# The chunk recurrence of a state-space layer: from a serial chain of steps to a rotated prefix scan

## The chip, the cores and the metric

The kernel runs on one core of one Trainium2 chip. The metric is the device time of one execution in microseconds (us); lower is better. Its engines are TensorE (PE; PEld is its weight load), VectorE (DVE), ScalarE (ACT), GpSimd (POOL) and SyncE (SP), which here only issues DMAs. Each engine works through its own instructions in order and waits on semaphores for the others.

## The reference, cut to what matters

One inference step of a two-layer decoder: 256 prompt tokens and 8 sequences of 8 sample tokens, 320 columns in all, model width 1024. Each layer is FFN 1, a token mixer, FFN 2 and a per-layer input embedding. The token mixer runs sliding-window attention and, beside it, a state-space recurrence (S5) with 32 groups of 16 channels and 64 complex states each:

```python
a_bar = jnp.exp(lam * dt)                        # one complex number per state
bu = jnp.einsum('gnp,blgp->lbgn', b_bar, ug)     # inputs of the states
if h0 is not None:
    bu = bu.at[0].add(a_bar * h0)
_, h = lax.associative_scan(_ssm_combine, (a, bu), axis=0)   # h_t = a_bar h_{t-1} + bu_t
y = jnp.einsum('gpn,lbgn->blgp', c, h).real.reshape(bt, l, SSM_W)
```

## The kernel before, in words

Tokens are the columns, features the 128 partitions. Every weight block is loaded as f32, split into a high part (`wh`, on ACT, line 162) and a low part (`wl`, on DVE, line 163), and each product takes three matmuls of 320 columns (lines 181 to 183). Up to three weight blocks are ready ahead of their use.

The recurrence is cut into chunks of 8 tokens: 32 chunks of the prompt and 8 of the samples, one per sequence. `chunk_in(gb)` (op `i` in the order string) transposes the inputs `u2` of 8 groups and multiplies them with a table into `Vt`, which holds for each state (128 partitions: 64 real parts, then 64 imaginary parts), each of 32 groups and each of 40 chunks what the chunk adds to the state. Then the state at the start of each chunk, `H`, follows from H[c+1] = A H[c] + V[c], with A the eighth power of `a_bar`. `chunk_out(gb)` (op `y`) multiplies U and H with two tables, `tt` and `wc`, into the outputs. The sample chunks take their start from `h0`.

Before, `scan` (op `h`) does this for all 32 groups after the last `chunk_in`: the 32 prompt chunks form 4 blocks of 8; `astep` (lines 636 to 645) makes one complex step for all 4 blocks at once with five DVE instructions, seven times in a row, then three steps across the blocks, then ten instructions (lines 678 to 683) that bring the block starts into every chunk. The powers of A that it needs, `gr` and `gi` with nine entries each, come from `prep`.

`prep(l)` makes the tables of a layer. It is a generator: `step(side)` runs it to its next `yield` after each of the 22 hidden blocks and each of the 16 output blocks of an FFN, 38 times. Layer 0's tables are made during layer 0's FFN 1, layer 1's during layer 0's FFN 2; what is left is run at the FFN's end. Its last part is eight DMAs on POOL's queue (line 553) that lay out the `tt` table in DRAM.

The order of the work in the mixer is written out in `MIXSEQ`: `p` projections, `i` and `y` as above, `s`, `f`, `m` the scores, transposes and products of six attention units, `t` and `w` loads of `tt` and `wc`, `z` the embedding's projections, `A` and `S` the output products. A planner takes the instructions in this order of preference and puts each engine's instructions in sequence, by its own estimate of when each is ready. The row scale of a norm is a power on POOL (line 248), which the evacuations of the projections (lines 596, 600, 603) need.

Of the kernel before, what the change touches and what calls it, by code (L numbers as in the profile page):

```python
# [12 lines left out]
AF = mybir.ActivationFunctionType  # L13
# [6 lines left out]
P = 128  # L20
# [14 lines left out]
MIXSEQ = 'w0 p0 p1 p3 i0 p2 i2 w1 i3 i1 p8 h0 t1 p9 v t2 p5 t0 e x p4 y0 s0 s1 w2 f0 p6 m0 p7 s2 f1 t3 m1 s3 f2 m2 y0 w3 y0 y1 s4 f3 y1 m3 s5 z0 f4 z1 y1 z2 z3 y2 f5 y2 y3 m4 y3 y2 z4 y3 z5 z6 m5 a g0 g1 A0 z7 n A1 A2 S0 S1 S2 A3 S3'  # L35
SCANS = ((0, 32),)
# [3 lines left out]
FXG = 16  # L40
# [9 lines left out]
def hybrid_step_kernel(ctx: ExitStack, tc, I, O):  # L50
# [138 lines left out]
    class Norm:  # L189
        """Statistics and split operand of an RMSNorm over nb feature blocks."""  # L190
# [46 lines left out]
        def finish(self, then=None):  # L237
            """Statistics of the row scale; its broadcast is left for later, behind a few products."""
# [138 lines left out]
    def prep(l):  # L377
# [53 lines left out]
        V.tensor_tensor(pr[:, 1, :], t, er, op=OP.mult)  # L431
        V.scalar_tensor_tensor(t, sn, 2.0, cs, op0=OP.mult, op1=OP.mult)
        V.tensor_tensor(pi[:, 1, :], t, er, op=OP.mult)
        yield
        powers(pr, pi)
        gr, gi = st("gr", (P, 9, G)), st("gi", (P, 9, G))
        V.tensor_copy(gr[:, 1, :], pr[:, 8, :])
        V.tensor_copy(gi[:, 1, :], pi[:, 8, :])
        powers(gr, gi)
        V.tensor_scalar(gi[64:128], gi[64:128], -1.0, None, op0=OP.mult)  # L440
        gtab.append((gr, gi))
# [115 lines left out]
    def mix(l, pre, post):  # L557
# [71 lines left out]
        gr, gi = gtab[l]  # L629
# [3 lines left out]
        nc.sync.dma_start(h0, I["h0"][l])  # L633

        def astep(out, hin, vin, k, n, gs):
            GH = gs.stop - gs.start
            t = st("sc1", (P, 128))[:, : GH * n].rearrange("p (g n) -> p g n", n=n)
            w = st("sc2", (P, 128))[:, : GH * n].rearrange("p (g n) -> p g n", n=n)
            V.tensor_tensor(t, hin, gr[:, k, gs].unsqueeze(2).to_broadcast([P, GH, n]), op=OP.mult)
            for a, b in ((0, 64), (64, 0)):  # L640
                V.tensor_tensor(w[a : a + 64], hin[b : b + 64],  # L641
                                gi[b : b + 64, k, gs].unsqueeze(2).to_broadcast([64, GH, n]),
                                op=OP.mult)
            V.tensor_tensor(t, t, vin, op=OP.add)  # L644
            V.tensor_tensor(out, t, w, op=OP.add)

        def scan(hh):
            g0, GH = SCANS[hh]
            gs = slice(g0, g0 + GH)
            Hh, Vh = H[:, gs], Vt[:, gs]  # L650
            Hp = Hh[:, :, 0:32].rearrange("p g (b k) -> p g b k", k=8)
            Vp = Vh[:, :, 0:32].rearrange("p g (b k) -> p g b k", k=8)
            lc = st("lc", (P, G, 4))[:, gs]
            sb = st("sb", (P, G, 4))[:, gs]

            PO.memset(Hp[:, :, :, 0], 0.0)
            V.tensor_copy(Hp[:, :, :, 1], Vp[:, :, :, 0])
            for k in range(1, 7):
                astep(Hp[:, :, :, k + 1], Hp[:, :, :, k], Vp[:, :, :, k], 1, 4, gs)
            astep(lc, Hp[:, :, :, 7], Vp[:, :, :, 7], 1, 4, gs)  # L660
            V.tensor_copy(sb[:, :, 0:1], lc[:, :, 0:1])
            for b in range(1, 4):
                astep(sb[:, :, b : b + 1], sb[:, :, b - 1 : b], lc[:, :, b : b + 1], 8, 1, gs)
            for f0 in range(g0, g0 + GH, FXG):
                fs = slice(f0, min(f0 + FXG, g0 + GH))
                ng = fs.stop - f0
                fx = auxt("s", [P, 2, ng, 3, 8])
                ft, fw = fx[:, 0], fx[:, 1]

                def gk(tile, p0, p1):  # L670
                    return tile[p0:p1, 0:8, fs].rearrange("p k g -> p g k").unsqueeze(2).to_broadcast(
                        [p1 - p0, ng, 3, 8])

                def sk(p0, p1):
                    return sb[p0:p1, f0 - g0 : fs.stop - g0, 0:3].unsqueeze(3).to_broadcast(
                        [p1 - p0, ng, 3, 8])

                V.tensor_tensor(ft, gk(gr, 0, P), sk(0, P), op=OP.mult)
                V.tensor_tensor(fw[0:64], gk(gi, 64, P), sk(64, P), op=OP.mult)
                V.tensor_tensor(fw[64:128], gk(gi, 0, 64), sk(0, 64), op=OP.mult)  # L680
                V.tensor_tensor(ft, ft, fw, op=OP.add)
                Hf = H[:, fs, 8:32].rearrange("p g (b k) -> p g b k", k=8)
                V.tensor_tensor(Hf, Hf, ft, op=OP.add)
            S.activation(Hh[:, :, 32:NC], h0[:, gs], AF.Copy)
            S.activation(fin[:, gs, 8:9], sb[:, :, 3:4], AF.Copy)
# [25 lines left out]
        class Prompt:  # L711
# [42 lines left out]
            def mix(self):  # L754
# [7 lines left out]
                cp(ya[:, self.m, 0:TP], po[:, 0:TP])  # L762

        class Sample:
            """Four of the sample sequences."""

            def __init__(self, tp):
                self.tp = tp
# [381 lines left out]
```

## Time and profile before

| what | before |
|---|---|
| median of 3 runs | 1305.47 us |
| lowest and highest run | 1303.61 and 1311.94 us |
| span of the profiled execution | 1307.1 us |
| PE busy | 1272.5 us, 97% |
| DVE busy | 894.7 us, 68% |
| ACT busy | 599.1 us, 46% |
| POOL busy | 72.7 us, 6% |

The profiled execution has no time beside its span; the span lies inside the range of the three runs and 1.6 us above their median. Busy shares are means over the span. The mixer of layer 0 runs from about 254 to 374 us, that of layer 1 from about 895 to 1015 us; the rest is FFNs and embedding. [...]

### The profile page before, as it was taken

The page shows a single profiled execution, that of the slowest core. Times are in us where ns is not written, and L with a number is a line of the kernel's source. Part 1 is how long each engine was busy: PE and PEld are TensorE (multiplying, and loading weights), DVE is VectorE, ACT ScalarE, POOL GpSimd, SP SyncE. Part 2 cuts the span into 40 slices and gives each one's busy share as a digit, 9 for nine tenths or more (in the row PEclk, how much of TensorE's full clock was granted, in tenths as well). Part 3 has the DMA queues.
Part 4 walks back from the last instruction along what each step waited for, and adds up shares of the span by engine and source line. Part 5 has one row for each costly group of instructions (what it writes and reads, how often), then busy time and mean ns, then how long its engine had stood idle before and what let it go on. Part 6 is the DMA issues. An engine that isn't in the chain of part 4 may idle for free.

```text
span 1307.1 us, 22973 instructions
## 1 busy us (share of the span) xinstructions
PE 1272.5 (97%) x9153; PEld 1241.5 (95%) x9153; DVE 894.7 (68%) x1583; ACT 599.1 (46%) x986; POOL 72.7 (6%) x92
## 2 busy tenths in 40 slices
PE   7999999998999999999999999999899999999996
PEld 7999999987899999999999999999778999999996
DVE  6588885758896978656875555566778755555575
ACT  5433434543864443334653334345357544334453
POOL 4300001000004000100000000000000000000000
PEclk9999999997999999999999999999979999999998
DMA  7836766652254467754554455345322444454351
GB/s 259 307 115 202 249 208 206 194 168 84 76 179 146 138 209 252 233 180 137 169 172 146 125 165 162 123 138 185 130 81 84 147 147 140 134 178 147 110 179 41
DMA packets 74619, 210.62 MB, mean 161 GB/s; under 512 B 8544, under 2 KB 18496, under 8 KB 74480
## 3 DMA queue, kind: packets, MB, share of 16 engines
q1 hardware_dynamic: 72560, 203.22, 48.6%
q0 software_dynamic: 1664, 5.28, 1.2%
q8 instruction: 72, 1.18, 0.4%
q10 hardware_dynamic: 288, 0.66, 0.1%
q14 instruction: 35, 0.29, 0.1%
HBM read 191.78 MB, written 19.69 MB: 162 GB/s over the span
## 4 chain that ended last, share of the span: by engine, by line
PE 91%; DVE 5%; issue 2%; ACT 0%; DMA 0%; POOL 0%; SPq 0%; POOLq 0%; DVEq 0%
PE pt L181 17%; PE pt L183 17%; PE pt L182 17%; PE pc L181 10%; PE pc L183 10%; PE pc L182 10%; PE pa L844 1%; DVE sc L641 1%; DVE wl L163 1%; PE pa L624 1%; PE pa L613 1%; PE pt L725 1%; PE pa L499 1%; PE pt L750 0%; DVE sc L644 0%
## 5 line engine op out<-in xcount | busy, mean ns | idle before, releaser
L162 ACT ACTIVATE wh<-wr 128x1024 fp32r<-128x1024 f32 (+3 forms) x365 | 351.1, 963 | 562.1 <-issue 284.0
L181 PE MATMUL pt<-big,wh 128*128 128x320 f32 x1584 | 491.6, 311 | 1.0 <-ACT big L228 1.0
L182 PE MATMUL pt<-big,wh 128*128 128x320 f32 x1584 | 490.8, 310 | 0.0
L183 PE MATMUL pt<-big,wl 128*128 128x320 f32 x1584 | 490.5, 310 | 0.2 <-DVE wl L163 0.2
L163 DVE TENSOR_TENSOR wl<-wr,wh 128x1024 fp32r<-128x1024 f32 (+3 forms) x365 | 403.4, 1108 | 111.8 <-ACT wh L162 110.2
L181 PE MATMUL pc<-big,wh 128*128 128x320 f32 x992 | 314.0, 317 | 6.8 <-ACT wh L162 5.9
L183 PE MATMUL pc<-big,wl 128*128 128x320 f32 x992 | 310.4, 313 | 0.0
L182 PE MATMUL pc<-big,wh 128*128 128x320 f32 x992 | 310.3, 313 | 0.0
L181 PEld LDWEIGHTS pt<-big,wh 128*128 128x128 f32 x1584 | 297.8, 188 | 2.0 <-ACT big L228 1.5
L183 PEld LDWEIGHTS pt<-big,wl 128*128 128x128 f32 x1584 | 297.7, 188 | 0.8 <-DVE wl L163 0.6
L182 PEld LDWEIGHTS pt<-big,wh 128*128 128x128 f32 x1584 | 297.9, 188 | 0.4
L181 PEld LDWEIGHTS pc<-big,wh 128*128 128x128 f32 x992 | 188.9, 190 | 11.3 <-ACT wh L162 5.9
L182 PEld LDWEIGHTS pc<-big,wh 128*128 128x128 f32 x992 | 189.1, 191 | 1.4 <-DVE big L225 1.2
L183 PEld LDWEIGHTS pc<-big,wl 128*128 128x128 f32 x992 | 188.9, 190 | 0.8 <-DVE wl L163 0.4
L290 DVE TENSOR_TENSOR fa<-pt,ft 128x320 f32<-128x320 f32 x88 | 43.1, 490 | 98.1 <-PE pt L183 97.9
L287 DVE TENSOR_TENSOR ft<-pc,r 128x320 f32<-128x320 f32 x88 | 42.9, 490 | 58.5 <-PE pc L183 58.4
L248 POOL TENSOR_TENSOR r<-ms,mhalf 107x3 f32<-107x3 f32 x13 | 13.4, 1032 | 734.8 <-DVE ms L246 734.8
L333 DVE SCALAR_TENSOR_TENSOR fd<-pt,r 128x320 f32<-128x320 f32 x64 | 31.4, 490 | 32.8 <-PE pt L183 32.8
L294 ACT ACTIVATE big<-fa 128x320 fp32r<-128x320 f32 x88 | 40.5, 460 | 20.0 <-DVE fa L290 19.7
L288 ACT ACTIVATE ft<-ft 128x320 f32<-128x320 f32 x88 | 40.0, 457 | 19.9 <-DVE ft L287 19.9
L224 ACT ACTIVATE big<-xa,prm 128x320 fp32r<-128x320 f32 x64 | 35.3, 559 | 22.7 <-DVE xa L334 9.8
L295 DVE TENSOR_TENSOR big<-fa,big 128x320 fp32r<-128x320 f32 x88 | 42.7, 485 | 2.7 <-ACT big L294 2.7
(236 smaller groups left out, 893.6 us busy)
## 6 DMA issues: line engine op xcount, KB each, us to landing
wr<-f1u SPq DMA_DIRECT2D x44, 512.0 KB, 3.4
wr<-f2g SPq DMA_DIRECT2D x44, 512.0 KB, 3.4
wr<-f2u SPq DMA_DIRECT2D x44, 512.0 KB, 3.3
wr<-f1g SPq DMA_DIRECT2D x43, 512.0 KB, 3.4
wr<-f1d SPq DMA_DIRECT2D x32, 384.0 KB, 3.2
wr<-f2d SPq DMA_DIRECT2D x32, 384.0 KB, 3.2
wr<-f1d SPq DMA_DIRECT2D x32, 320.0 KB, 2.9
wr<-win SPq DMA_DIRECT2D x20, 512.0 KB, 4.0
```

Of the source, the lines that this page charges most:

```text
L162: S.activation(h[:, c], raw[:, c], AF.Copy)
L163: i = V.tensor_tensor(lo[:, c], raw[:, c], h[:, c].bitcast(F32), op=OP.subtract)
L181: PE.matmul(ps, h[:, c], xh, start=start and k == 0, stop=False)
L182: PE.matmul(ps, h[:, c], xl, start=False, stop=False)
L183: PE.matmul(ps, lo[:, c], xh, start=False, stop=stop and k == n - 1)
L224: S.activation(h, src, AF.Copy, scale=g)
L287: V.tensor_tensor(t, pg, r, op=OP.mult)
L288: S.activation(t, t, AF.Silu)
L290: V.tensor_tensor(a, pu, t, op=OP.mult)
L294: S.activation(h, a, AF.Copy)
L295: V.tensor_tensor(lo, a, h.bitcast(F32), op=OP.subtract)
L333: V.scalar_tensor_tensor(t, pd, 0.5, r, op0=OP.mult, op1=OP.mult)
```

## The change

The recurrence of the prompt chunks becomes one prefix scan per group on DVE (`tensor_tensor_scan`: state = decay * state + input, along the columns). A complex state can't go through it directly, so V is first turned by minus c times the phase of A for chunk c: in that frame the recurrence has the real factor |A|. The result is turned back into `H[c+1]`, and the last one into `fin`. `rotate(gb)` (op `r`) does this for 8 groups at a time, so that it can follow each `chunk_in`; `h0` in the order string is gone, and `r0`, `r2`, `r3`, `r1` stand behind `i2`, `i3`, `p8`, `r3`. The 8 groups lie one behind the other in a row of 256 columns, and the decay is 0 at the first column of each. The cosines and sines of c times the phase (`ect`, `est`, 32 chunks by 32 groups) and the decays (`dec`, filled on POOL) are made in `prep` by doubling, brought back to length 1 in two halves, and kept; the powers of A beyond the first are no longer made. `prep` gets six more `yield`s. The final states of the samples are made in one pass over 32 groups where there were two of 16. The builder is given `dynamic_dma_scratch_size=4096`. Comments are removed.

```diff
+MIXSEQ = 'w0 p0 p1 p3 i0 p2 i2 r0 w1 i3 r2 i1 p8 r3 r1 t1 p9 v t2 p5 t0 e x p4 y0 s0 s1 ...'
-MIXSEQ = 'w0 p0 p1 p3 i0 p2 i2 w1 i3 i1 p8 h0 t1 p9 v t2 p5 t0 e x p4 y0 s0 s1 ...'
...
         powers(pr, pi)
-        gr, gi = st("gr", (P, 9, G)), st("gi", (P, 9, G))
-        V.tensor_copy(gr[:, 1, :], pr[:, 8, :])
-        V.tensor_copy(gi[:, 1, :], pi[:, 8, :])
-        powers(gr, gi)
-        V.tensor_scalar(gi[64:128], gi[64:128], -1.0, None, op0=OP.mult)
-        gtab.append((gr, gi))
+        gr, gi = st("gr"), st("gi")
+        V.tensor_copy(gr, pr[:, 8, :])
+        V.tensor_copy(gi[0:64], pi[0:64, 8, :])
+        V.tensor_scalar(gi[64:128], pi[64:128, 8, :], -1.0, None, op0=OP.mult)
+        yield
+        for k in range(3):
+            V.tensor_tensor(er, er, er, op=OP.mult)
+        dec = st("dec", (P, G, NB))
+        PO.tensor_copy(dec, er.unsqueeze(2).to_broadcast([P, G, NB]))
+        PO.memset(dec[:, :, 0:1], 0.0)
+        ct_, sn_ = st("ect", (P, G, NB)), st("est", (P, G, NB))
+        PO.memset(ct_[:, :, 0:1], 1.0)
+        PO.memset(sn_[:, :, 0:1], 0.0)
+        for k in range(3):
+            V.tensor_tensor(t, us, us, op=OP.mult)
+            V.scalar_tensor_tensor(us, us, 2.0, uc, op0=OP.mult, op1=OP.mult)
+            V.tensor_scalar(uc, t, -2.0, 1.0, op0=OP.mult, op1=OP.add)
+        V.tensor_copy(ct_[:, :, 1], uc)
+        V.tensor_copy(sn_[:, :, 1], us)
+        yield
+        for m in (1, 2, 4, 8, 16):
+            n = min(m, NB - 1 - m)
+            shp = [P, G, n]
+            a1, a2 = ct_[:, :, m : m + 1].to_broadcast(shp), sn_[:, :, m : m + 1].to_broadcast(shp)
+            b1, b2 = ct_[:, :, 1 : n + 1], sn_[:, :, 1 : n + 1]
+            q1, q2 = auxt("s", [P, G, n]), auxt("s", [P, G, n])
+            q3, q4 = auxt("p", [P, G, n]), auxt("p", [P, G, n])
+            V.tensor_tensor(q1, a1, b1, op=OP.mult)
+            V.tensor_tensor(q2, a2, b2, op=OP.mult)
+            V.tensor_tensor(q3, a1, b2, op=OP.mult)
+            V.tensor_tensor(q4, a2, b1, op=OP.mult)
+            V.tensor_tensor(ct_[:, :, m + 1 : m + n + 1], q1, q2, op=OP.subtract)
+            V.tensor_tensor(sn_[:, :, m + 1 : m + n + 1], q3, q4, op=OP.add)
+            if m > 4:
+                yield
+        for c0 in (0, 16):
+            cc, ss = ct_[:, :, c0 : c0 + 16], sn_[:, :, c0 : c0 + 16]
+            q1, q2 = auxt("s", [P, G, 16]), auxt("p", [P, G, 16])
+            V.tensor_tensor(q1, cc, cc, op=OP.mult)
+            V.tensor_tensor(q2, ss, ss, op=OP.mult)
+            V.tensor_tensor(q1, q1, q2, op=OP.add)
+            V.tensor_scalar(q1, q1, -0.5, 1.5, op0=OP.mult, op1=OP.add)
+            V.tensor_tensor(cc, cc, q1, op=OP.mult)
+            V.tensor_tensor(ss, ss, q1, op=OP.mult)
+            yield
+        V.tensor_scalar(sn_[64:128], sn_[64:128], -1.0, None, op0=OP.mult)
+        gtab.append((gr, gi, ct_, sn_, dec))
         yield
...
-        def scan(hh):
...
+        PO.memset(H[:, :, 0:1], 0.0)
+        S.activation(H[:, :, NB:NC], h0, AF.Copy)
+
+        def rotate(gb):
+            gs = slice(gb * 8, gb * 8 + 8)
+            v = Vt[:, gs, 0:NB]
+            c, z = ect[:, gs], est[:, gs]
+            tg = auxt("s", [P, 3, 8, NB])
+            t, w, g = tg[:, 0], tg[:, 1], tg[:, 2]
+
+            def turn(src):
+                V.tensor_tensor(t, src, c, op=OP.mult)
+                V.tensor_tensor(w[0:64], src[64:128], z[64:128], op=OP.mult)
+                V.tensor_tensor(w[64:128], src[0:64], z[0:64], op=OP.mult)
+
+            turn(v)
+            V.tensor_tensor(t, t, w, op=OP.subtract)
+            V.tensor_tensor_scan(g.rearrange("p g c -> p (g c)"),
+                                 dec[:, gs].rearrange("p g c -> p (g c)"),
+                                 t.rearrange("p g c -> p (g c)"), 0.0, OP.mult, OP.add)
+            turn(g)
+            V.tensor_tensor(H[:, gs, 1:NB], t[:, :, 0 : NB - 1], w[:, :, 0 : NB - 1], op=OP.add)
+            V.tensor_tensor(fin[:, gs, 8:9], t[:, :, NB - 1 : NB], w[:, :, NB - 1 : NB], op=OP.add)
...
-            "p": proj, "i": chunk_in, "h": scan,
+            "p": proj, "i": chunk_in, "r": rotate,
...
-    nc = _bacc.Bacc("TRN2", target_bir_lowering=False, num_devices=1)
+    nc = _bacc.Bacc("TRN2", target_bir_lowering=False, num_devices=1,
+                     dynamic_dma_scratch_size=4096)
```

## Rows read from the trace of the kernel before

**Rows 1.** The page: the span, and PE's busy time, share, instructions.

```profile
span 1307.1 us, 22973 instructions
PE 1272.5 (97%) x9153; PEld 1241.5 (95%) x9153; DVE 894.7 (68%) x1583; ACT 599.1 (46%) x986; POOL 72.7 (6%) x92
```

**Rows 2.** Stretches of both mixers: start:end, length, busy by engine, clock, DMA.

```profile
270.00:286.00 16.00, 15.85 (x193) 13.73 (x192) 3.91 (x5) 8.47 (x16) 0.56 (x1) 1.00 0.62 203
286.00:322.00 36.00, 29.31 (x174) 25.98 (x173) 32.51 (x79) 8.91 (x15) 1.50 (x3) 0.81 0.23 73
300.50:307.50 7.00, 5.75 (x23) 5.18 (x24) 6.52 (x21) 0.00 (x0) 0.00 (x0) 0.53 0.25 77
314.50:321.20 6.70, 6.39 (x36) 5.00 (x37) 5.85 (x12) 0.98 (x2) 0.95 (x2) 0.50 0.07 10
322.00:354.00 32.00, 31.81 (x339) 26.66 (x338) 26.07 (x63) 28.41 (x85) 2.62 (x6) 1.00 0.29 99
925.00:968.00 43.00, 35.79 (x226) 31.79 (x225) 37.24 (x88) 12.97 (x31) 1.70 (x4) 0.80 0.28 95
940.00:946.50 6.50, 5.54 (x29) 5.33 (x30) 6.03 (x21) 0.81 (x1) 0.00 (x0) 0.74 0.25 83
952.60:965.40 12.80, 12.11 (x79) 9.73 (x80) 9.94 (x21) 5.00 (x19) 0.97 (x2) 0.51 0.24 84
```

**Rows 3.** PE's waits over the whole span: total us, times, longest.

```profile
PE pt L725 <- DVE big L600: 5.6, 2, 2.8
PE pa L844 <- DVE big L683: 5.3, 2, 2.9
PE pt L701 <- DVE kv L603: 3.0, 2, 1.5
```

**Rows 4.** Timeline of PE, layer 0: start, length, instruction, idle time before it and releaser.

```profile
301.75 1.23 PE L725 MATMUL pt<-kv,big 64*128 64x256 f32 x4 [2.82 <-DVE big L600]
...
314.81 0.65 PE L844 MATMUL pa<-wc,big 128*40 128x128 f32 x4 [2.39 <-DVE big L683]
```

**Rows 5.** Timeline of DVE, layer 0: start, length, instruction (first, one between, last).

```profile
285.83 0.29 DVE L657 COPY big<-big 128x128 f32<-128x128 f32 x1 [3.74 <-ACT big L83]
...
289.81 0.48 DVE L603 TENSOR_TENSOR kv<-pt,r 128x320 f32<-128x320 f32 x1
...
317.03 0.55 DVE L683 TENSOR_TENSOR big<-big,s 128x384 f32<-128x384 f32 x1
```

**Rows 6.** Timeline of ACT, layer 0: the first and last of four copies into `Vt`.

```profile
269.62 0.44 ACT L83 ACTIVATE big<-pa 128x320 f32<-128x320 f32 x1 [1.71 <-PE pa L624]
...
285.36 0.44 ACT L83 ACTIVATE big<-pa 128x320 f32<-128x320 f32 x1 [1.42 <-PE pa L624]
```

**Rows 7.** Groups of DVE instructions by shape: busy us, mean ns, idle before.

```profile
L359 DVE TENSOR_TENSOR cm<-pwr 128x32 f32<-128x32 f32 x1 | 0.2, 185 | 0.0
L739 DVE TENSOR_TENSOR s<-s,dn 128x256 f32<-128x256 f32 x4 | 1.7, 418 | 0.0
L463 DVE TENSOR_TENSOR sx<-kc,qr 128x512 f32<-128x512 f32 x1 | 0.7, 687 | 0.0
L857 DVE SCALAR_TENSOR_TENSOR big<-big,prm,pa 128x320 f32<-128x320 f32 x4 | 3.3, 816 | 0.6 <-PE pa L855 0.6
```

**Rows 8.** Stretches of the FFNs, columns as in Rows 2.

```profile
80.00:110.00 30.00, 30.00 (x209) 29.99 (x208) 29.81 (x93) 11.66 (x17) 0.00 (x0) 1.00 0.36 96
60.00:258.00 198.00, 198.00 (x1402) 196.30 (x1402) 154.79 (x303) 85.20 (x123) 5.63 (x10) 1.00 0.64 198
700.00:860.00 160.00, 160.00 (x1093) 160.00 (x1092) 85.45 (x116) 60.04 (x84) 0.00 (x0) 1.00 0.46 141
```

**Rows 9.** Timeline of POOL, layer 0, and landing times of line 553's DMAs.

```profile
209.00 4.85 POOL L553 DMA_DIRECT2D ttd<-ktd  x8 [8.42 <-DMA ktd<-kc]
260.99 0.88 POOL L248 TENSOR_TENSOR r<-ms,mhalf 107x3 f32<-107x3 f32 x1 [47.13 <-DVE ms L246]
DMA to landing us min/median/max: 3.2/5.8/6.2
```

More of the change, by code (lines that the diff above doesn't have):

```diff
@@ L34 @@
 WB = 4
-MIXSEQ = 'w0 p0 p1 p3 i0 p2 i2 w1 i3 i1 p8 h0 t1 p9 v t2 p5 t0 e x p4 y0 s0 s1 w2 f0 p6 m0 p7 s2 f1 t3 m1 s3 f2 m2 y0 w3 y0 y1 s4 f3 y1 m3 s5 z0 f4 z1 y1 z2 z3 y2 f5 y2 y3 m4 y3 y2 z4 y3 z5 z6 m5 a g0 g1 A0 z7 n A1 A2 S0 S1 S2 A3 S3'
-SCANS = ((0, 32),)
+MIXSEQ = 'w0 p0 p1 p3 i0 p2 i2 r0 w1 i3 r2 i1 p8 r3 r1 t1 p9 v t2 p5 t0 e x p4 y0 s0 s1 w2 f0 p6 m0 p7 s2 f1 t3 m1 s3 f2 m2 y0 w3 y0 y1 s4 f3 y1 m3 s5 z0 f4 z1 y1 z2 z3 y2 f5 y2 y3 m4 y3 y2 z4 y3 z5 z6 m5 a g0 g1 A0 z7 n A1 A2 S0 S1 S2 A3 S3'
 ABUFS = {"s": 2, "p": 2, "qs": 1, "kc": 1, "vc": 1, "sx": 2, "pj": 1}
@@ L39 @@
 KCUT = 7
-FXG = 16
+NB = 32
 HEAD = 2
@@ L430, in prep @@
         V.tensor_scalar(t, t, -2.0, 1.0, op0=OP.mult, op1=OP.add)
-        V.tensor_tensor(pr[:, 1, :], t, er, op=OP.mult)
-        V.scalar_tensor_tensor(t, sn, 2.0, cs, op0=OP.mult, op1=OP.mult)
-        V.tensor_tensor(pi[:, 1, :], t, er, op=OP.mult)
+        uc, us = st("uc"), st("us")
+        V.tensor_copy(uc, t)
+        V.tensor_tensor(pr[:, 1, :], uc, er, op=OP.mult)
+        V.scalar_tensor_tensor(us, sn, 2.0, cs, op0=OP.mult, op1=OP.mult)
+        V.tensor_tensor(pi[:, 1, :], us, er, op=OP.mult)
@@ L627, in chunk_in @@
             cp(Vt[:, gb * 8 : gb * 8 + 8, :], pv[:, : 8 * NC].rearrange("p (g c) -> p g c", g=8))
-        gr, gi = gtab[l]
+        gr, gi, ect, est, dec = gtab[l]
         H = bigt([P, G, NC])
@@ L633, in mix @@
         nc.sync.dma_start(h0, I["h0"][l])
[L635 to L645, printed above, removed]
@@ L647, in scan @@
-        def scan(hh):
[L648 to L685, printed above, removed]
@@ L923, in mix @@
             ops[o[0]](int(o[1:] or 0))
-        for f0 in range(0, G, 16):
-            fs = slice(f0, f0 + 16)
-            astep(fin[:, fs, 0:8], h0[:, fs], Vt[:, fs, 32:NC], 1, 8, fs)
+        shp = [P, G, 8]
+        ft = auxt("s", [P, 2, G, 8])
+        V.tensor_tensor(ft[:, 0], h0, gr.unsqueeze(2).to_broadcast(shp), op=OP.mult)
+        for a, b in ((0, 64), (64, 0)):
+            V.tensor_tensor(ft[a : a + 64, 1], h0[b : b + 64],
+                            gi[b : b + 64].unsqueeze(2).to_broadcast([64, G, 8]), op=OP.mult)
+        V.tensor_tensor(ft[:, 0], ft[:, 0], Vt[:, :, NB:NC], op=OP.add)
+        V.tensor_tensor(fin[:, :, 0:8], ft[:, 0], ft[:, 1], op=OP.add)
         PO.dma_start(O["hf"][l], fin)
```

## The prediction

> **What bounds the kernel now.** I began with the page's first part: PE is busy for 1272.5 of 1307.1 us [rows 1]. So the kernel is bound by TensorE nearly everywhere, and a change on DVE can win only where PE waits for DVE, or where those waits have cost PE its clock. PE's list of waits says where that is. Its three largest waits on DVE [rows 3] all lie in the mixers, once per layer each: for the evacuation of v's projection (line 603, 1.5 us), for that of q's (line 600, 2.8 us) and for the finished states (line 683, 2.9 us at most). None of the first two is long work by itself. DVE's timeline shows what stands in front of them: the scan runs from 285.83 to 317.58 us in layer 0, 31.7 us with other work threaded in, and line 603 sits in the middle of it [rows 5]. DVE is busy for 32.51 of the 36 us from 286 to 322, while ACT has 8.91 [rows 2]. So here DVE is the bound, not PE.
>
> The stretches of both mixers give the price. In layer 0, PE is idle for 36 - 29.31 = 6.7 us, in layer 1 for 43 - 35.79 = 7.2 us [rows 2]. [...] Work at half clock takes twice its time, so half of it is lost: about 2.8 + 3.2 = 6.0 us in layer 0. In layer 1 the first stretch is at half clock for only about half of its length: 5.54 x (1 - 0.74) = 1.4 us, and the second loses 12.11 x 0.49 = 5.9 us; 7.3 in all. The whole price of the scan's place is 6.7 + 6.0 + 7.2 + 7.3 = 27.2 us. That is the most that the removal can give.
>
> **The change, part by part.**
>
> *The scan itself.* One `rotate` has ten DVE instructions: three to turn, one subtraction, the prefix scan, three to turn back, one sum into H, one small sum into `fin`. Eight of them have 256 columns; the nearest row is 128x256 at 418 ns [rows 7], also for those of 64 partitions, since partitions run side by side. That is 8 x 0.418 = 3.3 us; the small one is 0.185 us at most, by the 128x32 row. The prefix scan has no row. Its lower bound is an ordinary instruction of its shape, 0.42 us; its upper bound is the slowest of like length in the mixer, 0.82 us for line 857 [rows 7]. I take 0.42, since shape and operands are those of that row. So a `rotate` is 3.9 us, up to 4.3, and four are 15.8 to 17.4 us, all instructions counted at full length.
> [...]
>
> *Its place.* The four copies into `Vt` come from 269.62 to 285.36 us [rows 6]. In the 16 us from 270 to 286 DVE is busy for only 3.91 [rows 2], so 12 us are free and three `rotate`s (11.8 us) fit there; a half of the third may slip behind. Behind the last copy at 285.8 stand `r1`, 3.9 us, and at most 2 us of leftover, instead of 31.7 us. DVE is then free from about 290 to 292. PE's wait for v ends as line 603 ends, at 290.3 [rows 5], so PE wants v from 288.8 on; its evacuation can be threaded into `r1`, as it was threaded into the scan. The waits on lines 600 and 683 ended at 301.75 and 314.81 [rows 4]: both go, since DVE is free 10 us before. What is late next in these places: v's evacuation, for which I keep 0.7 us of PE's wait per layer (between 0 and the 1.5 of today), and the attention units, whose chain of scores, exponentials and transposes now starts some 12 us earlier. From 322 to 354 PE is busy for 31.81 of 32 us, ACT for 28.41 and DVE for 26.07 [rows 2]: all three are nearly full there, but ACT had almost nothing to do in the 36 us before. PE's remaining projections now fill the time of the first unit's softmax. I keep 1.5 us per layer for gaps in it (between 0 and a whole lost wait of 2.8). Neither gap should lower the clock: the mean of 0.81 from 286 to 322 is a loss of 36 x 0.19 = 6.8 us, which the two stretches behind the waits of 2.82 and 2.39 us make up alone (7 x 0.47 + 6.7 x 0.5 = 6.6) [rows 2, 4]; the wait of 1.5 us cost none.
>
> *The tables.* Per layer `prep` loses the powers of `gr` (18 small instructions of 32 to 128 columns, 4.1 us between the rows) and gains three squarings, nine instructions of angle doubling, three copies (15 x 0.185 = 2.8 us), the doublings of 1, 2, 4, 8 and 16 columns by 32 groups (six instructions each, between the rows at about 0.185, 0.22, 0.28, 0.42, 0.66: 10.6 us), the renormalization (12 x 0.687 = 8.2 us [rows 7]) and a change of sign (at most 1.2 us). Net: 22.8 - 4.1 = 18.7 us of DVE in each of two FFNs. The FFN with layer 0's tables has DVE busy for 154.79 of 198 us [rows 8], so 43 us are free over its length. It is not spread evenly: from 80 to 110 DVE is full, 29.81 of 30 us, and yet PE loses nothing there and issues 209 matmuls in 30 us, 7.0 per us against 6.8 in a stretch without tables [rows 8]. Weight splits run three blocks ahead, three times 24 matmuls or 10 us, and that absorbs the lag. A hidden block takes 48 matmuls, 6.9 us; at the 53% of the table-free stretch (85.45 of 160 [rows 8]) DVE has 3.2 us of it left for a piece of `prep`. Today a piece of some 24 x 0.185 = 4.4, one of 8.5 and one of 7.5 us follow each other, and the lag grows to 1.2 + 5.3 + 4.3 = 10.8 us. After, pieces of 4.4, 4.6, 2.7, 6.6, 4.0, 4.1, 4.1, 1.2 and 7.5 us give 39.2 - 9 x 3.2 = 10.4 us; with five of them in output blocks, where I allow 0.8 us less room each, 14 us. I take no cost for PE. The cover is the weight queue, and if it fails it is the 3 to 4 us of difference and a fall of the clock worth 3 us: 0 to 7 us.
>
> *What the six yields move.* 38 steps no longer run `prep(0)` out, so its last DMAs are issued at FFN 1's end, and all behind the new steps comes six steps later. The eight DMAs of line 553 at 209.00 [rows 9] move by two hidden blocks of 6.9 and four output blocks of 30 matmuls, 4.3 us each: to about 240. On POOL's queue line 248 at 260.99 comes next, and the loads of `tt` on SP follow behind the rotations. With 4.85 us to issue and 6.2 us to land [rows 9] they end at about 251: free, with 10 us in hand for DVE's lag. SP's loads of the attention cache move by as much, into the last blocks of FFN 1, and are needed only by the attention units. The filling of `dec` on POOL has nothing behind it for 100 us.
>
> *Small things.* ACT loses one small copy; the sample's final states lose six instructions, off the path: 0.
>
> Sum on the profiled execution: 1307.1 - 27.2 + 2 x (0.7 + 1.5) = 1284.3 us. The span is 1.6 us above the median of the runs, so for a median I say **1283 us**.
>
> **The rivals.**
>
> *1. Another wait takes the place (20%).* The planner may put the rotations late, or in front of the u and v evacuations and weight splits that PE needs at once (a rotation queued before its copy into `Vt` holds up all behind it on DVE), and the attention units may keep PE waiting once per layer. For it: from 270 on DVE would be over 90% full, and ACT is at 28.41 of 32 us in the stretch that moves forward. Against it: PE has 7 us of projections to fill. Price: per layer one wait of 2.8 us and one half-clock stretch of 3.0 us stay, 11.6 us: about 1294.
>
> *2. Slower: the tables break the FFNs (9%).* DVE is already full from 80 to 110 us. If the lag passes what the prepared weights cover, PE waits for `wl` us for us: 2 x 18.7 = 37 us, and two or three falls of the clock of 3 us each: 45 us against 23 won, about 1328. It decides from a lag of 11 us on, which today's pieces reach without a loss. Against it: the new pieces are finer, and by the mean slack they end at 10.4.
>
> *3. POOL's queue (6%).* If the eight table DMAs are held up, line 248 behind them is late, and with it every projection of layer 0's mixer. One at a time, at 5.8 us each [rows 9], they would end 46 us after 240, 25 us behind line 248's time, and the clock falls once: about 1283 + 28 = 1311; two at a time they end at 263 and cost 2 us.
> [...]
>
> *4. It does not do what it says (4%).* Rotations all land behind 286 us and are as long as the scan: 1305.
>
> **The numbers.** My forecast has 61%, with a range of its own from 1276 (all 27.2 us, from the lowest run) to 1291 (7 us for the tables). Rival 1 reaches from 1288 to 1300. The range of 1276 to 1300 holds 61 + 19 and the milder half of rival 3, about 8 in 10. About 1% is what a measurement of this kernel tells from no change: below 1292.4 lie the forecast and half of rival 1: 0.71. Above 1318.5 lies rival 2: 0.09. The rest is 0.20.
>
> **What would show it.** In the profile after: ten DVE instructions per `rotate`, the prefix scan at 0.42 to 0.82 us; three rotations before 286 us; PE's waits on lines 600 and 683 gone and that on 603 at most 1.5 us; the granted clock at 1.00 from 286 to 322 and from 925 to 968; PE full in both FFNs with tables; line 553 done before line 248. It is wrong if PE waits for `wl` between 60 and 200 us, if line 248 starts late, or if a wait over 2.5 us turns up in the attention units.

## The result and the profile after

| | before | after |
|---|---|---|
| median of the runs on one chip (4 each) | 1306.97 us | 1290.94 us |
| lowest and highest | 1303.61, 1311.94 us | 1289.31, 1292.73 us |
| span of the profiled execution | 1307.1 us | 1290.9 us |

The ratio after/before is 0.9881, 95% interval 0.986 to 0.9903: faster by 1.2%, a small difference, but clear of 1. The time is 8 us above the prediction of 1283, at the upper end of the forecast's own range (1276 to 1291) and inside the whole range. The head of the page after (beside [rows 1]):

```profile
span 1290.9 us, 22996 instructions
PE 1260.0 (98%) x9153; PEld 1232.9 (96%) x9153; DVE 910.4 (71%) x1609; ACT 599.7 (46%) x984; POOL 78.0 (6%) x96
```

PE has lost 12.5 us of busy time with the same number of matmuls, and its mean granted clock over the span has risen from 0.985 to 0.992 (1.00 is full speed): fewer of them ran at half clock. DVE has become busier (910.4 us against 894.7) and the kernel faster: what counted was where its work stands. The line numbers have shifted: 248 is now 247, 553 is 595, 596, 600 and 603 are 638, 642 and 645. The stretches of [rows 2] and [rows 8] in the trace after:

```profile
254.00:286.00 32.00, 25.94 (x166) 24.21 (x166) 13.85 (x19) 11.34 (x14) 2.30 (x3) 0.88 0.50 178
286.00:322.00 36.00, 34.94 (x354) 30.75 (x352) 30.86 (x67) 18.63 (x43) 2.39 (x5) 0.97 0.38 123
...
925.00:968.00 43.00, 42.01 (x395) 37.30 (x393) 36.36 (x77) 29.09 (x80) 3.73 (x6) 1.00 0.36 127
60.00:258.00 198.00, 196.97 (x1395) 195.10 (x1393) 167.02 (x340) 83.63 (x121) 7.85 (x13) 1.00 0.60 194
375.00:640.00 265.00, 265.00 (x1865) 263.24 (x1864) 211.03 (x403) 118.06 (x172) 22.03 (x22) 1.00 0.57 188
```

Layer 1's stretch (the third line) is as forecast: PE 42.01 of 43 us at clock 1.00, where it had 35.79 at 0.80. Layer 0's mixer is nearly full from 286 on (34.94 of 36 us, 29.31 before), but has a new hole just before: 25.94 of 32 us at 0.88. Before, that stretch had none:

```profile
254.00:286.00 32.00, 31.69 (x331) 28.79 (x330) 12.58 (x17) 16.02 (x27) 2.62 (x4) 1.00 0.56 186
```

Both FFNs with tables (the last two lines of the block before) have DVE busier by 12.2 and 13.4 us (before, the second had 197.59). PE is full in the second and idle for 1.0 of 198 us in the first, at its very end: the table work is hidden. PE's waits (the four that matter):

```profile
PE pa L655 <- DVE big L638: 3.6, 3, 3.3
PE pc L180 <- ACT big L223: 3.4, 2, 2.0
...
PE pt L739 <- DVE big L642: 0.5, 1, 0.5
PE pt L715 <- DVE kv L645: 0.4, 1, 0.4
```

Of the three waits of [rows 3] one is gone and two are down to 0.5 us at most. Two others have come up, both in layer 0. To see what each stretch won or lost, take the starts of the row-scale power (line 247) in POOL's timeline. It runs once ahead of each part of a layer, so the distance of two of them is the time of a part. All runs that follow are in this table (us, from the profiled executions; the last column is the median of the runs). The ratios given with the runs are to the kernel before as it ran beside each (medians 1305.9 to 1309.3), and a run that adds or removes lines shifts the line numbers by a few.

| run | FFN 1, layer 0 | mixer, layer 0 | FFN 2, layer 0 | mixer, layer 1 | median of the runs |
|---|---|---|---|---|---|
| before | 236.4 | 137.2 | 239.8 | 139.4 | 1307 |
| after | 241.0 | 130.2 | 239.8 | 123.9 | 1290.9 |
| e1 tables early | 245.4 | 124.0 | 239.8 | 123.9 | 1291.5 |
| e2 six empty steps, before | 238.2 | 149.5 | 239.8 | 136.4 | 1318.3 |
| e3 Toeplitz on SP | 232.5 | 147.0 | 252.9 | 123.9 | 1313.6 |
| e4 reserve 8192 | 240.5 | 128.4 | 239.8 | 123.9 | 1290.0 |
| e5 six steps merged | 245.7 | 124.0 | 256.7 | 123.9 | 1307.0 |
| e6 the same, rotations called later | 245.4 | 123.9 | 256.2 | 123.8 | 1306.3 |
| e7 no Toeplitz DMAs, layer 0 | 236.5 | 124.3 | 239.8 | 123.9 | 1282.3 |
| e8 zero fill later | 236.4 | 124.0 | 239.8 | 123.9 | **1281.6** |
| e9 small Toeplitz rows | 237.2 | 124.3 | 239.8 | 123.9 | 1282.2 |
| e10 e8, rotations behind last copy | 236.4 | 132.3 | 239.8 | 132.0 | 1296.9 |
| e11 e8, rotations twice | 236.3 | 130.6 | 239.8 | 131.1 | 1295.1 |
| e12 both | 236.3 | 142.5 | 239.8 | 142.4 | 1318.1 |

Layer 1's mixer won 15.5 us. Layer 0's won only 7.0, and FFN 1 ahead of it lost 4.6: 2.4 us in all where 10.5 were forecast. That is the question of the experiments. The chain that layer 0 shows, first on POOL:

```profile
242.61 4.86 POOL L595 DMA_DIRECT2D ttd<-ktd  x8 [5.10 <-DMA ktd<-kc]
...
266.33 0.89 POOL L247 TENSOR_TENSOR r<-ms,mhalf 107x3 f32<-107x3 f32 x1 [18.69 <-DVE ms L245]
```

The Toeplitz DMAs come at 242.6 (predicted: about 240; before 209.0), and the power at 266.3 in place of 260.99 [rows 9]. Then the DMAs issued from 225 to 262 us (issues, KB of one, median us to landing):

```profile
wr<-win SPq DMA_DIRECT2D x8, 512.0 KB, 6.3
wr<-f1d SPq DMA_DIRECT2D x7, 320.0 KB, 4.2
...
kc<-kc SPq DMA_DIRECT2D x1, 512.0 KB, 9.8
...
ttd<-ktd POOLq DMA_DIRECT2D x1, 256.0 KB, 5.8
...
ttd<-ktd POOLq DMA_DIRECT2D x1, 32.0 KB, 8.3
```

In the same stretch before:

```profile
wr<-win SPq DMA_DIRECT2D x9, 512.0 KB, 4.2
wr<-f1d SPq DMA_DIRECT2D x6, 320.0 KB, 2.8
```

From 243 to 255 us the DMA engines are now full, a share of 1.00 at 354 GB/s, and ACT waits for both kinds of weights (its waits from 225 to 270 us):

```profile
ACT wh L161 <- DMA wr<-win: 4.4, 3, 2.3
...
ACT wh L161 <- DMA wr<-f1d: 3.7, 3, 2.0
```

One `win` block takes 9.5 us to land (before, at most 4.4). ACT's timeline has the wait for it:

```profile
255.06 1.06 ACT L161 ACTIVATE wh<-wr 128x1024 fp32r<-128x1024 f32 x1 [2.27 <-DMA wr<-win]
```

DVE splits that block at 256.15, in front of the residual sum that FFN 1's output is waiting for. PE's timeline shows where that ends:

```profile
258.95 0.41 PE L180 MATMUL pc<-big,wh 128*128 128x320 f32 x1 [1.98 <-ACT big L223]
...
276.55 0.44 PE L265 MATMUL pa<-ident,r 107*128 107x107 f32 x3
...
280.26 1.03 PE L655 MATMUL pa<-ident,big 128*40 128x128 f32 x8 [3.28 <-DVE big L638]
```

The first of these lines is FFN 1's loss: PE waits 1.98 and, a microsecond later, 0.59 us, and its mean clock is 0.81 from 258 to 267 us, where some 13 matmuls of 320 columns start 0.267 us apart in place of 0.147; that makes about 4.1 of the 4.6 us. The last is the hole in the mixer: u's evacuation (line 638) needs the row scale `r`, `r` needs the spread (line 265), and the spread stands in PE's order 57 matmuls later than before. The power was done at 267.2; PE ran the spread only at 276.55. Before, it came a microsecond behind the power:

```profile
262.84 0.44 PE L266 MATMUL pa<-ident,r 107*128 107x107 f32 x3
```

So PE waits for u, its clock falls (0.72 from 278 to 286, 0.85 from 286 to 294), and the first rotation starts at 287.9.

### The profile page after: what moved, and what is told of

It reads as the page before. It is cut to its first block, busy times and chain, and to the rows that moved or that the text cites. A ratio compares the mean times of both kernels' runs of the same rounds, so it can differ in the third digit from the quotient of the medians.

```text
span 1290.9 us, 22996 instructions
## 1 busy us (share of the span) xinstructions
PE 1260.0 (98%) x9153; PEld 1232.9 (96%) x9153; DVE 910.4 (71%) x1609; ACT 599.7 (46%) x984; POOL 78.0 (6%) x96
## 4 chain that ended last, share of the span: by engine, by line
PE 72%; DVE 3%; issue 2%; POOL 1%; ACT 1%; POOLq 0%; DVEq 0%; ACTq 0%
PE pt L180 14%; PE pt L181 14%; PE pt L182 14%; PE pc L180 9%; PE pc L182 9%; PE pc L181 9%; PE pa L858 1%; DVE wl L162 1%; POOL r L247 1%; PE pa L666 0%; PE po L773 0%; PE pa L869 0%; DVE s L690 0%; DVE s L689 0%; PE pt L764 0%
## 5 line engine op out<-in xcount | busy, mean ns | idle before, releaser
L293 ACT ACTIVATE big<-fa 128x320 fp32r<-128x320 f32 x88 | 40.4, 460 | 18.5 <-DVE fa L289 18.3
```

The costliest lines, as they stand in the source:

```text
L293: S.activation(h, a, AF.Copy)
```

## The experiments

My theory after the result (A): the six new yields push the last DMAs of layer 0's tables into the end of FFN 1, where they hold up weights and move the spread; the rotations themselves are as good in layer 0 as in layer 1. The rivals: B, the rotations, threaded between the copies, hold layer 0's mixer up; C, the smaller `dynamic_dma_scratch_size` holds POOL's DMAs up, a form of the prediction's third rival.

### e1: the tables as early as before

```diff
         if l == 0:
-            yield
-            yield
             zt = wpool.tile([P, 1024], F32, ...)
...
                 nc.sync.dma_start(tt_d[ll]..., zt...)
-                yield
...
             nc.sync.dma_start(sinks, I["sinks"])
-            yield
...
         PO.tensor_tensor(er, econ, zr, op=OP.pow)
         yield
         yield
-        yield
+        if l:
+            yield
```

> The changed kernel, but prep(0) gives up six of its older yields (two at its start, two in the loop that fills with zeros, one behind the masks, one of the three empty ones), so that everything behind the new tables is issued as early in FFN 1 as before the change; the tables and the mixer are those of the change. In this build's order the spread of the mixer's row scale stands 57 matmuls earlier on PE, where the kernel before has it. Theory A (six steps too late): layer 0 lost its gain because the last DMAs of the tables and of the attention cache ran into the end of FFN 1. Then the power of line 247 comes at about 261 (266.3 in the changed kernel), three rotations are done by about 288, the mixer's waits of 3.3 us and the fall of the clock from 278 to 294 go, and the time falls by 8 to 12 us to 1279 to 1283. Theory B (the rotations themselves, threaded between the copies and evacuations, hold layer 0's mixer up): about 1291, no change. [...] Against all: pieces of the tables that are now in the first, fullest blocks could make PE wait there, 3 to 7 us.

Measured: 1291.52 us, ratio to before 0.9889 (0.987 to 0.9908): no faster than the change. The median alone would have spoken for theory B. The parts say otherwise: layer 0's mixer takes 124.0 us, as layer 1's, and the waits there are gone, while FFN 1 takes 9 us more than before. That loss is at its start (a stretch):

```profile
30.00:60.00 30.00, 23.06 (x144) 22.40 (x144) 19.09 (x71) 11.12 (x16) 10.03 (x9) 0.89 0.90 323
```

The wait in PE's timeline:

```profile
43.80 0.63 PE L180 MATMUL pc<-big,wh 128*128 128x320 f32 x1 [6.58 <-ACT wh L161]
```

With 4 MB of zeros and the loads of the tables issued at once, PE waits 6.6 us for a weight. So B is refuted, and the first yields of `prep` turn out to be what keeps those 4 MB from standing in front of the weights.

### e2: six empty steps in the kernel before

```diff
         gtab.append((gr, gi))
         yield
+        for _ in range(6):
+            yield
```

> The kernel before, with nothing but six empty yields in prep where the change puts its six new ones. No table work is added and the scan is the old one. Theory A: the power of line 248 comes 4 to 6 us later than its 260.99, PE's order puts the spread 57 matmuls later, and the kernel is slower by 5 to 12 us: 1312 to 1319. Theories B and C: no change, 1307.

Measured: 1318.25 us, ratio 1.0097 (1.0079 to 1.0115), 12 us slower with nothing added but lateness. The power comes only 1.8 us later on FFN 1's own count; the expected 4 to 6 did not show. The mixer loses 12.4 us, and its spread runs at 272.22 (PE's timeline) against 262.84:

```profile
272.22 0.44 PE L266 MATMUL pa<-ident,r 107*128 107x107 f32 x3
```

The six steps alone cost the kernel before 12 us, three quarters of the 16 that the whole change gave. In the changed kernel the loss is smaller (about 10 us, e7 to e9); that its shorter DVE work makes up for a part is likely, but no run shows it.

### e3: the Toeplitz DMAs on SP's queue

```diff
-            PO.dma_start(dst[:, :, i * 16 :], src[:, :, : (8 - i) * 16])
+            nc.sync.dma_start(dst[:, :, i * 16 :], src[:, :, : (8 - i) * 16])
```

> The changed kernel, with the eight Toeplitz DMAs of line 595 issued on SP's queue instead of POOL's, as late as the change has them. POOL's queue then has nothing in front of the power of line 247, and in this build's order PE's spread stands 120 matmuls earlier than in the changed kernel; but the same bytes still move at the end of FFN 1, now in line with the weight loads. If the loss comes from POOL's queue and from the place of the spread that follows from it: 1281 to 1285. If it comes from the DMA engines being full at 243 to 255, so that the last weight loads are late: the mixer's weights are later still, PE waits at the start of the mixer, 1290 to 1296. Theory B: 1291.

Measured: 1313.59 us, ratio 1.0059 (1.0042 to 1.0076): worse than all of the expectations. The spread runs early, at 257.66, so its place does follow those DMAs. But PE now waits for a weight of the mixer (PE's timeline):

```profile
280.65 0.64 PE L182 MATMUL pt<-big,wl 128*128 128x320 f32 x1 [4.04 <-DVE wl L162]
```

It is not the weight's transfer that is late. The four `win` loads issued from 251.1 to 262.6 us land in 3.1 to 5.9 us, the last at 266.8. Their splits stand in ACT's order behind a copy that waits for PE's transposes (ACT's timeline):

```profile
271.07 1.07 ACT L82 ACTIVATE sx<-pa 40x512 f32<-40x512 f32 x2 [9.96 <-PE pa L655]
...
274.93 3.88 ACT L161 ACTIVATE wh<-wr 128x1024 fp32r<-128x1024 f32 x4
```

Layer 0's FFN 2, with layer 1's tables, loses 13 us in the same way: at its end, weights that landed 5 us and more before wait for their split behind other work of ACT. So the DMAs cost here through the order that the planner gives the engines, as with the spread, and the expectation that weights would land too late in the mixer did not show. FFN 1 and the mixer together take 379.5 us, 371.2 in the change; one by one they don't compare, since in e3 the power stands 48 matmuls earlier on PE.

### e4: 8192 bytes of DMA scratch

```diff
-                     dynamic_dma_scratch_size=4096)
+                     dynamic_dma_scratch_size=8192)
```

> The changed kernel with 8192 bytes in place of 4096 for the DMA scratch; every engine's order is the same. [...] Theories A and B: 1291, the issues at 4.86 us.

Measured: 1289.96 us, ratio 0.9879 (0.9862 to 0.9896); the change itself has 0.9881. The issues take 4.84 us against 4.86 (POOL's timeline):

```profile
241.80 4.84 POOL L595 DMA_DIRECT2D ttd<-ktd  x8 [5.36 <-DMA ktd<-kc]
```

By theory C the issues would get shorter or start earlier, the power would start before 266 us, and the time would fall by 3 us or more. With 8192 bytes they are 0.02 us shorter; they start 0.8 us earlier and the power 1.6 us (264.74), but in both traces what POOL waits for in front of them is `ktd`, whose wait is no shorter (5.36 us against 5.10), and the time is only 1.0 us lower, less than the spread of either kernel's runs. So theory C is out, and no run here shows a cost of 4096 bytes.

### e5 and e6: six steps merged, and the rotations called later

```diff
         PO.tensor_tensor(er, econ, zr, op=OP.pow)
         yield
-        yield
-        yield
...
         V.tensor_scalar(gi[64:128], pi[64:128, 8, :], -1.0, None, op0=OP.mult)
-        yield
...
         V.tensor_copy(sn_[:, :, 1], us)
-        yield
...
-            if m > 4:
+            if m > 8:
                 yield
...
         gtab.append((gr, gi, ct_, sn_, dec))
-        yield
```

> The changed kernel, with six yields of prep given back where they cost the start of the kernel nothing: two of the three empty ones behind the powers, and four of the new pieces of the tables joined to their neighbours (the one behind gi, the one behind the doubled angle, the one at m = 8, the one behind gtab); the first steps with their zero fill and loads stay where they are, and the pieces of DVE's work in the tables get larger. Both layers. Theory A (the last DMAs of the tables come six steps too late, and the run with everything early paid for its gain at 30 to 60 us): no wait at 30 to 60 us, line 247 at about 261, PE's 3.3 us wait before the mixer and the half clock behind it gone, 1279 to 1283. Theory D (whatever layer 0's mixer gains is lost again in FFN 1, since the table work must be done there anyway): 1288 to 1292.

e6 adds one more line:

```diff
-... p2 i2 r0 w1 i3 r2 i1 p8 r3 r1 t1 ...
+... p2 i2 w1 i3 i1 p8 r0 r2 r3 r1 t1 ...
```

> The kernel of the run before it in this list, with the four rotations called together where the scan was called (behind p8), instead of between the first projections and copies. Theory P (the early place gives most of the gain: the rotations run before v and q need DVE): the wait for v's evacuation and that for q's come back in part, 15.8 us of rotations stand in front of them, and each mixer loses 3 to 6 us: 1287 to 1293. Theory L (the shorter scan gives it, 17 us in place of 31.7, wherever it stands): within 2 us of that kernel, 1279 to 1285.

Measured: e5 1306.97 us, ratio 0.9989 (0.9974 to 1.0004); e6 1306.25, 0.9987 (0.9972 to 1.0002). The whole gain is lost, and neither of the times expected of e5 was met. Layer 0's mixer is whole (124.0 us), but the FFNs are not: 9 us in the one, 17 in the other. In both PE waits for weight splits, and once for a table instruction (`kk`) itself; FFN 2's waits (395 to 640 us, e5):

```profile
PE pt L182 <- DVE wl L162: 4.8, 1, 4.8
PE pt L180 <- ACT wh L161: 2.9, 3, 1.6
PE pc L180 <- DVE kk L409: 1.8, 1, 1.8
PE pc L182 <- DVE wl L162: 1.4, 1, 1.4
```

This is the mechanism of the prediction's second rival, which I gave 9%, at work as soon as the pieces are larger: the joined piece is 18 us by the prediction's own prices, past the 10.8 us of lag that by its estimate are borne without loss. So the yields were needed, and their number is what pushes the end back. e6 was to tell place from length and could not: the first prefix scan starts 11.4 us behind the power in both, because the planner puts a rotation where its copy is ready, whatever the order string says. e10 to e12 replace it.

### e7 and e9: without the transfers, or with small ones

```diff
-            PO.dma_start(dst[:, :, i * 16 :], src[:, :, : (8 - i) * 16])
+            if l or i == 7:
+                PO.dma_start(dst[:, :, i * 16 :], src[:, :, : (8 - i) * 16])
```

> The changed kernel without seven of the eight Toeplitz DMAs of layer 0 (the 16-wide one stays, so layer 0's tables of that kind are left mostly zero). The six steps stay late, and so do the loads of the attention cache; 1.1 of the some 10 MB that move from 225 to 262 us go, and POOL's queue is nearly free; in this build's order the spread of the row scale stands where the kernel before has it. If the late Toeplitz DMAs are the cause, the changed kernel's loss in layer 0 goes: 1279 to 1284, line 247 at 261 to 262. If it is the late loads of the cache and the weights behind them: 1288 to 1292, line 247 at 265 to 266.

```diff
-            PO.dma_start(dst[:, :, i * 16 :], src[:, :, : (8 - i) * 16])
+            PO.dma_start(dst[:, :, 112:], src[:, :, :16])
```

> The changed kernel with all eight Toeplitz DMAs of both layers still issued on POOL, 512 rows each, but each only 16 columns wide (so the tables are mostly zero): 0.26 MB in place of 1.15 MB per layer, with the same number of rows. In this build's order the spread of the row scale stands where the kernel before has it. If the loss in layer 0 comes from the bytes on the DMA engines, and from the place that the planner gives the spread because of their transfer time: 1279 to 1284. If it comes from POOL's issues (4.86 us) or from the number of rows: 1287 to 1291, and line 247 at 265 to 266.

Measured: e7 1282.27 us, ratio 0.9799 (0.9769 to 0.9829); e9 1282.15, 0.9799 (0.9771 to 0.9826). The six steps are as late as in the change, the cache loads too, and the loss is gone: the power is at 262.18 and 261.75, the spread back at 264.05 and 263.61 (PE's timeline of e7):

```profile
264.05 0.44 PE L265 MATMUL pa<-ident,r 107*128 107x107 f32 x3
```

That of e9:

```profile
263.61 0.44 PE L265 MATMUL pa<-ident,r 107*128 107x107 f32 x3
```

So the whole loss of layer 0 hangs on the late Toeplitz transfers, and in e9 on their size, not on POOL's issues or the number of rows. Two effects are left that these runs take away together: the weights that land late, and the place of the spread. The traces part them by time. FFN 1's 4.6 us arise before the power, which stands behind the same 1737 matmuls before and after, so the spread can't have made them: they are the weight that landed late. The mixer's other 6 us come behind it. In the runs that give the spread its old place and leave the rotations as they are, the mixer takes 123.9 to 124.3 us, also in e9, where `win` still lands only after 6.0 us; with the 57 matmuls in front it takes 128.4 (e4) and 130.2, and e2 has the same wait of 3.3 us. No run moves the spread alone, so this part is argued from the order of events.

### e8: the six steps from a place that costs nothing

```diff
-        if l == 0:
-            yield
-            yield
-            ...  (zero tile, zero fill of both layers, masks, with three yields)
         lam = st("lam", (P, 3, G))
...
         yield
         yield
-        yield
+        for _ in range(1 * l):
+            yield
...
         gtab.append((gr, gi, ct_, sn_, dec))
         yield
+        if l == 0:
+            zt = auxt("qs", [P, 512])
+            PO.memset(zt, 0.0)
+            nc.sync.dma_start(tt_d[0]..., zt...)
...
         V.tensor_copy(bst[64:128], bb[64:128, 1])
         yield
+        if l == 0:
+            nc.sync.dma_start(tt_d[1]..., zt...)
+            ...  (masks)
```

> The changed kernel with the pieces of the tables as the change has them, one DVE piece per step, but six steps given back at the front: the loads for the tables and the powers on POOL come first, without the two yields ahead of them, the zero fill of both layers' Toeplitz tables (4 MB) and the masks move from the start to two steps in the middle of FFN 1 (from a zero tile of 512 columns), and one of the three empty yields goes. Theory A, sharpened by the runs so far (late Toeplitz DMAs cost 8.7 us in layer 0; a crowded start costs 10; merged pieces of tables cost 5 us in one FFN and 17 in the other): none of the three prices is paid; no wait at 30 to 60 us, PE full from 60 to 240, line 247 at 261 to 263, layer 0's mixer 80 to 81 us long as layer 1's: 1279 to 1284. If DVE has no room for the tables so early, or the 4 MB are in the way of the weights at their new place: a wait of 3 to 7 us for wl or wh between 60 and 200 us, and 1285 to 1292.

Measured: 1281.56 us, ratio 0.9791 (0.9763 to 0.9818), with the full computation: the fastest kernel here, 2.1% under before and 0.9% under the change (0.9791/0.9881). DVE is full at the start and PE loses nothing by it; the stretch with the mixer's start is full too:

```profile
30.00:60.00 30.00, 30.00 (x207) 30.00 (x206) 29.49 (x110) 12.70 (x19) 8.68 (x11) 1.00 0.47 156
...
254.00:286.00 32.00, 31.66 (x330) 28.76 (x329) 22.59 (x42) 15.31 (x25) 2.30 (x3) 1.00 0.53 172
```

### e10 to e12: place against length

What in the scan was the price: that it stood behind the last copy, or that it was long? Two edits on e8, alone and together. The first makes every rotation depend on the last copy; the second does each rotation twice.

```diff
+        def tie(k):
+            V.tensor_scalar(ect[:, :, 0], Vt[:, 8, 0:G], 0.0, 1.0, op0=OP.mult, op1=OP.add)
-... i2 r0 w1 i3 r2 i1 p8 r3 r1 t1 ...
+... i2 w1 i3 i1 k r0 r2 r3 r1 p8 t1 ...
```

```diff
+            for _ in range(2):
-            turn(v)
+                turn(v)
...
```

> The kernel of run e8 with one small DVE instruction more per layer: it writes the ones in the cosine table's first column again, from a value that the last copy into Vt has brought, so that no rotation can begin before that copy; all four rotations then stand between it and the evacuation of v in DVE's order, in one stretch of 15.8 to 17 us. (Calling them later by name did not move them: in run e6 the planner put them where they were.) Theory P (the early place, between the copies, gives most of the gain): v's evacuation comes 10 to 12 us later, PE waits for it and for q's, with a fall of the clock, 3 to 6 us per mixer: 1288 to 1293 against e8's 1281.6. Theory L (DVE's shorter work gives it, wherever it stands): within 2 us of e8.

> The kernel of run e8 with each rotation done twice (same result): 33 us of DVE work per layer, about what the scan took (31.7 us with other work in it), but still in four parts that begin as soon as their copy is there. Theory P: most of the gain stays, since half of the work is done before the last copy: within 4 us of e8. Theory L: the gain goes, each mixer is back at 90 to 96 us, 1300 to 1310.

> Both: rotations twice and none before the last copy. DVE's work is as long and stands where the scan of the kernel before did. By both theories the gain goes: each mixer 94 to 98 us as in the kernel before, 1306 to 1312. If it stays under 1295, neither length nor place was what the scan cost.

Measured: e10 1296.93 us, ratio 0.9903 (0.9889 to 0.9918); e11 1295.08, 0.9891 (0.9876 to 0.9906); e12 1318.14, 1.0066 (1.0049 to 1.0082). Per mixer, against 124.0: 8.2 us for the place, 6.8 for the length, 18.5 for both. Each theory expected one of the two to be nearly free; neither is. DVE's timeline says why. v's evacuation, in e8 behind the third rotation:

```profile
284.58 0.69 DVE L693 TENSOR_TENSOR_SCAN s<-dec,s 128x256 f32<-128x256 f32 x1
...
288.39 0.49 DVE L644 TENSOR_TENSOR kv<-pt,r 128x320 f32<-128x320 f32 x1
...
290.27 0.68 DVE L693 TENSOR_TENSOR_SCAN s<-dec,s 128x256 f32<-128x256 f32 x1
```

The same evacuation in e10:

```profile
299.06 0.47 DVE L644 TENSOR_TENSOR kv<-pt,r 128x320 f32<-128x320 f32 x1
```

And PE's timeline of e10, with the wait for it:

```profile
299.59 0.90 PE L717 MATMUL pt<-ident,kv 128*128 128x128 f32 x3 [3.68 <-DVE kv L644]
```

DVE's timeline of e11:

```profile
298.85 0.49 DVE L644 TENSOR_TENSOR kv<-pt,r 128x320 f32<-128x320 f32 x1
```

PE's of e11:

```profile
299.40 0.90 PE L715 MATMUL pt<-ident,kv 128*128 128x128 f32 x3 [3.67 <-DVE kv L644]
```

Two different edits put v's evacuation off by nearly the same time (10.7 and 10.5 us) and cost PE the same wait, 3.7 us, and 8.2 and 6.8 us in all. Behind the wait PE's clock is at 0.50 (e10, a stretch):

```profile
300.00:306.00 6.00, 6.00 (x28) 5.22 (x27) 5.09 (x10) 1.21 (x3) 0.76 (x2) 0.50 0.28 94
```

In e12 it is no longer v but q's evacuation, with twice the work in front of it, that PE waits for, 10.2 us (line 641 there; PE's timeline):

```profile
313.86 0.63 PE L180 MATMUL pc<-big,wh 128*128 128x320 f32 x1 [10.16 <-DVE big L641]
```

So the gain of the change is neither "fewer instructions" nor "earlier" by itself. It is that DVE is free when PE asks for v and q.

## Why the prediction was right, and where its sum was wrong

*The price of the scan's place, 27.2 us: right, and a little short.* The clock is back at 1.00 in layer 1, and the waits of [rows 3] are gone or at most 0.5 us. In e8, free of the side effect, the mixers are 13.2 and 15.5 us shorter than before, 28.7 in all, where 27.2 was called the most that the removal can give; the span is 27.3 us below before (1279.8 against 1307.1). e12, with rotations that are late and twice as long, gives it all back and 9 us more. Its DVE work is longer than the scan's: the rotations add up to 33.7 us in a mixer, the scan's 63 instructions to 24.5 (31.7 was its length with other work threaded in). The clock's part of the price was counted from the four short stretches of [rows 2], as if work at half clock took twice its time. That factor was an estimate, and no run shows it: back-to-back matmuls of 320 columns (lines 181 to 183 of the kernel before) start 0.147 us apart at a clock of 1.00 (from 100 to 105 us) and 0.267 at 0.50 (from 305 to 307), 1.8 times.

*What takes the place, 4.4 us: too much.* v's wait in layer 1 is 0.4 us, where 0.7 was kept; none of PE's waits for the attention units is longer than 0.5 us, where 1.5 us of gaps were kept. Layer 1's mixer won 15.5 us where 12.3 were forecast.

*A rotation, 3.9 us: slightly short.* The groups of DVE instructions, eight of each:

```profile
L694 DVE TENSOR_TENSOR_SCAN s<-dec,s 128x256 f32<-128x256 f32 x8 | 5.5, 684 | 0.2
...
L688 DVE TENSOR_TENSOR s<-big,ect 128x256 f32<-128x256 f32 x8 | 3.4, 425 | 9.1 <-ACT big L82 9.0
...
L689 DVE TENSOR_TENSOR s<-big,est 64x256 f32<-64x256 f32 x8 | 3.4, 420 | 0.1
...
L699 DVE TENSOR_TENSOR fin<-s 128x8 f32<-128x8 f32 x8 | 1.4, 170 | 0.0
```

I took 0.42 us for the prefix scan; it takes 0.684, so a rotation is 4.2 us, inside the bound of 4.3, and four are 16.9. That the scan costs no more than an ordinary instruction of its shape was my assumption, and it did not hold: it takes 1.6 times a product. That an instruction on 64 partitions costs what one on 128 does held: 420 ns against 425. The scan's 0.26 us change about 0.3 us per layer.

*Tables at no cost: right.* FFN 2 takes 239.8 us before and after, and FFN 1 is back at 236.4 in e8. The price of 18.7 us holds too: the table instructions of an FFN add up to 58.2 us before and 76.8 after, 18.6 more. DVE's busy time rises by less, 12.2 and 13.4 us, because many of these instructions begin before the one ahead has ended (from 102.4 us in the trace after, products of 128x480 take 0.65 us and start 0.57 apart), and busy time counts that overlap once. The rival "tables break the FFNs" did not come about, but e5 shows how near it was: with the same work in larger pieces it takes the whole gain.

*Three rotations before 286 us: wrong in layer 0*, where the first starts at 287.9, and nearly right where the side effect is away (e8: prefix scans at 271.98, 278.81 and 284.58, so the third rotation is about half done at 286, as was allowed for).

*What the six yields move: this step failed.* It put the cost of the six later steps at nothing: it said that the late DMAs of line 553 are "free, with 10 us in hand", and that the cache loads, being needed late, cost nothing. The times were right (issued at 242.6, forecast 240; landed at about 255, forecast 251). The question was wrong: I asked when those transfers are needed, not what they pass on the way. They fall on the last weights of FFN 1 and the first of the mixer, one of which took 9.5 us to land, and the planner's place for the spread follows them. Of the signs of being wrong that the prediction named, one came: the power starts 5.3 us late. It was not held up in POOL's queue, as the third rival had it, but waited for DVE and so for FFN 1. Layer 0 was forecast at 10.5 us and gave 2.4; e7, e8 and e9 bring FFN 1 and the mixer from 371.2 to between 360.4 and 361.5 us, which is the missing 8 us and 2 more. Layer 1 has no such loss: its tables have no zero fill ahead of them, and their last Toeplitz DMA is issued at 595.8, 40 us before its FFN ends. The direction is the mechanism's, but that the time lies inside the forecast's own range is partly luck: layer 1 gave 3 us more than forecast and made up for part of the 8 that layer 0 gave less. I had a wait that "takes the place" among the rivals at 20%, and POOL's queue at 6%; the first is the nearer, but neither named the mechanism.

## What to carry to other kernels

A step that is moved later is priced by what it meets there, not by when its result is needed: look up what the DMA queues and the order of the engines hold at its new time. Where a planner orders the engines by its estimates, a late transfer also moves instructions that don't need it (the spread here, the weight splits in e3). Where a gain seems lost in one of two equal stages, time the stages one by one: e1 and the change have the same total and lost it in different places. Work in the shadow of another engine has two limits that pull against each other, the size of a piece (e5) and the number of pieces (e2); room for more pieces comes from moving bulk transfers out of the front (e8), not from merging.

## What the runs showed of the hardware

- A prefix scan of 128x256 f32 on DVE takes 684 ns, 1.6 times a product of that shape (421 to 425 ns in the rotations). A product of 64x256 takes 418 to 420 ns.
- With the Toeplitz DMAs (1.15 MB in rows of at most 512 B) and the cache loads beside them, weight loads of 512 KB land in 6.3 us at the median and 9.5 at most; with the cache loads and seven of the eight left out, in 4.6 (e7); with one transfer of 480 KB out of the cache beside them, in 4.2 (before). With the eight at 0.26 MB but as many rows they still take 6.0 (e9).
- The DMA engines' share alone says little: 0.88 of 30 us at the start went without a wait (before), 0.90 with one of 6.6 us (e1). By the edit, what differs is that e1 issues both 2 MB fills and the loads behind them in one step, ahead of the weight that PE needs.
